# An attention kernel: VectorE's share of the exponentials regrouped from three blocks in every second job to four in every fourth, and Q transposed one job ahead instead of two

## The chip, the cores and the metric

One core of a Trainium2 chip runs the whole program. The metric is device time in microseconds (us) of one launch. The engines named below are TensorE (PE, its weight loads PEld), VectorE (DVE), ScalarE (ACT), GpSimd (POOL) and SyncE (SP). Each works through its own instructions in the order in which the program issues them, and waits on semaphores for the others.

## The reference

Grouped-query attention, batch 8, sequence 512, 32 query heads, 8 key/value heads, head size 64, all float32:

```python
K_expanded = np.repeat(K, heads_per_group, axis=2)     # 4 query heads share one key head
scores = np.einsum('bhqd,bhkd->bhqk', Q, K_expanded) * scale
weights = np.exp(scores - np.max(scores, axis=-1, keepdims=True))
weights = weights / (np.sum(weights, axis=-1, keepdims=True) + 1e-10)
output = np.einsum('bhqk,bhkd->bhqd', weights, V_expanded)
```

## The kernel before

**Jobs and blocks.** The work is 64 jobs, j = 0 to 63. A job is one key head of one batch with its four query heads, taken as two pairs of heads (i = 0, 1; `DPAIR` is pair 1). The scores of a pair are made transposed, keys on the partitions: for each of four chunks of 128 keys (kc) and each head of the pair (m) a block of 128 keys x 512 queries. A job has 16 blocks. The exponential is taken without subtracting the maximum. Checks on the sums and on V set a flag, and a general path stands behind it for inputs that need it.

**Two engines take exponentials.** ACT takes most blocks in tiles of two (`act_tile`, ACTIVATE on L217, 128 x 1024), out of a pool of two PSUM buffers (`s_ps`): PE can write tile n's scores (L199) only when ACT has finished tile n-2. DVE takes the first `taken(j)` blocks of pair 1 (kc 0 first, then kc 1) by integer arithmetic on the bits of a float16 number:

- `exp_d` (scores into `d_ps` on L199, then u, L228),
- `exp_d2` (f, L249, the low bits of u),
- g (L241) and w (L245), the correction; for jobs 3 to 62 both run on POOL,
- `exp_d4` (L262), u + w, written to the tile `pt` beside ACT's results. It is issued one job later.

`taken(j)` is 2, and 3 where `WIDE(j)` holds: the even jobs from 10 on, 27 of them. A narrow job leaves ACT seven tiles of two blocks, a wide job six and a half (its tile 4 has one block).

**Order within job j**, written out by hand in the last loop of `fast_path`; `last` is job j-1, and pv(last, i, lo, hi) are products lo to hi of the 32 that multiply pair i's weights with V (L293), in the chunk order kc 2, 3, 1, 0, so that products 0 to 15 of pair 1 need ACT's blocks alone and products 16 to 31 the chunks in which DVE has a part. PE's queue is:

1. tile 0's scores, DVE's first two blocks, tile 1's scores,
2. pv(last, 0, 0, 16), tile 2, pv(last, 0, 16, 32), tile 3,
3. eight transposes of Q (L164, `trans_q`), tile 4,
4. pv(last, 1, ...) in three pieces, with tile 5 and tile 6 between them, and DVE's third block of job j+1 after tile 5 where j+1 is wide.

DVE's queue in the same job is: u(j); a check of V in some jobs (`check_v`, L173); the normalisation of (last, 0) (reciprocal L336, multiply L340); the copy of the transposed Q out of PSUM (L167); `exp_d4(last)`; f(j); u of the third block of j+1 where j+1 is wide; the normalisation of (last, 1). POOL's queue is g(j), w(j), then the DMA issues that the program writes at the head of job j+1 (loads of Q, K and V).

**PSUM.** The eight banks are two buffers of two banks for ACT's tiles, one buffer of two banks for `d_ps` (DVE's blocks and the transposes share it, one tile after the other), and one of two banks for `pv`. As there is one `pv` buffer, pv(last, 1) starts only after the normalisation of (last, 0), and pv(j, 0) in the next job only after that of (last, 1).

**Q ahead.** Up to job 6 the Q of job j+1 is transposed in job j. Job 7 transposes Q of jobs 8 and 9, and from job 8 on it is Q of j+2, into half of a `d_ps` tile. The other half takes the third block of a wide job j+1.

Of the kernel before, what the change touches and what calls it, by code (L numbers as in the profile page):

```python
# [13 lines left out]
FP16 = mybir.dt.float16  # L14
# [3 lines left out]
ALU = mybir.AluOpType  # L18
# [6 lines left out]
EXP_K = 3.28614867e-04  # L25
EXP_F1 = 1045.05112
# [7 lines left out]
V_HI = 1.0e15  # L34


WIDE = lambda j: j >= 10 and j % 2 == 0


@with_exitstack  # L40
# [18 lines left out]
def fast_path(ctx, tc, Q, K, V, out, flag):  # L59
    nc = tc.nc  # L60
    B, S, H, D = Q.shape
# [3 lines left out]
    GP = KV // 2  # L65
# [13 lines left out]
    dve_pool = ctx.enter_context(tc.tile_pool(name="dve", bufs=2))  # L79
# [78 lines left out]
    def trans_q(j, bank, lo=0, hi=NPAIR):  # L158
        u, g = divmod(j, 2)
        ps = bank.bitcast(BF16).rearrange("p (i sc c) -> p i sc c", i=NPAIR, sc=SC)  # L160
        for i in range(lo, hi):
            for sc in range(SC):
                h = g * HPG + 2 * i
                nc.tensor.transpose(ps[:, i, sc, :], qn[u][:, sc, h:h + 2, :], ident)  # L164
        if u not in qt:
            qt[u] = qt_pool.tile([128, 2, NPAIR, S], BF16, name="qt")
        return lambda: nc.vector.tensor_copy(  # L167
            out=qt[u][:, g, lo:hi, :], in_=ps[:, lo:hi, :, :].rearrange("p i sc c -> p i (sc c)")
        )

    def check_v(b, sc):
        n = b * SC + sc
        nc.vector.tensor_reduce(  # L173
            out=okv[:, n:n + 1], in_=vt[b % 2][:, sc, :, 0:D], op=ALU.max, axis=AX.XY,
            apply_absolute_value=True,
        )
# [3 lines left out]
    NJOB = NU * 2  # L180
    DPAIR = NPAIR - 1

    def taken(j):
        return 3 if WIDE(j) else 2

    def act_tiles(j):
        every = [(i, kc, m) for i in range(NPAIR) for kc in range(SC) for m in range(2)]
        first = DPAIR * SC * 2
        mine = [n for n in range(len(every)) if not first <= n < first + taken(j)]
        groups = [[n for n in mine if n // 2 == h] for h in range(len(every) // 2)]  # L190
        return [[every[n] for n in group] for group in groups if group]

    jobs, osb, invs, ends = {}, {}, {}, []

    def scores(j, ps, i, kc, m):
        u, g = divmod(j, 2)
        b, gp = divmod(u, GP)
        keys = kt_first[:, gp, :, :] if b == 0 else kt[b][:, :, gp, :]
        nc.tensor.matmul(  # L199
            ps,  # L200
            keys[64 * m:64 * m + 64, g ^ m, kc * 128:(kc + 1) * 128],
            qt[u][64 * m:64 * m + 64, g, i, :],
            start=True,
            stop=True,
        )
# [5 lines left out]
    def act_tile(j, n):  # L211
        group = act_tiles(j)[n]
        i, kc, lo = group[0]
        ps = s_pool.tile([128, 2, S], FP32, name="s_ps")
        for _, _, m in group:
            scores(j, ps[:, m, :], i, kc, m)
        nc.scalar.activation(  # L217
            out=jobs[j]["pt"][:, i, kc, lo:, :], in_=ps[:, lo:, :], func=EXP, scale=scale
        )

    def exp_d(j, lo, hi, ps):
        st = jobs.setdefault(j, {})
        if "u" not in st:
            for name, dtype in (("u", I16), ("f", I16), ("g", BF16), ("w", BF16)):
                st[name] = dve_pool.tile([128, 3, S], dtype, name=name + "16")[:, 0:taken(j), :]
        for n in range(lo, hi):
            scores(j, ps[:, n - lo, :], DPAIR, n // 2, n % 2)
        return lambda: nc.vector.tensor_scalar(  # L228
            out=st["u"][:, lo:hi, :], in0=ps[:, 0:hi - lo, :], scalar1=A_U, scalar2=B_U,
            op0=ALU.mult, op1=ALU.add,  # L230
        )


    def by_pool(j):
        return 3 <= j < NJOB - 1

    def correction(engine, f, g, w):
        as_bits = engine is nc.gpsimd  # L240
        engine.tensor_scalar(  # L241
            out=g, in0=f, scalar1=-EXP_F1, scalar2=EXP_K * 2.0 ** (24 * as_bits),
            op0=ALU.add, op1=ALU.mult,
        )
        engine.tensor_tensor(out=w, in0=g, in1=f.bitcast(FP16) if as_bits else f, op=ALU.mult)  # L245

    def exp_d2(j):
        st = jobs[j]
        nc.vector.tensor_single_scalar(  # L249
            out=st["f"], in_=st["u"], scalar=1023, op=ALU.bitwise_and  # L250
        )
        if by_pool(j):
            exp_d3(j, nc.gpsimd)

    def exp_d3(j, engine):
        st = jobs[j]
        correction(engine, st["f"], st["g"], st["w"])

    def exp_d4(j):
        st = jobs[j]  # L260
# [17 lines left out]
    def pv(j, i, lo, hi):  # L278
        st = jobs[j]
        u, g = divmod(j, 2)  # L280
        b, gp = divmod(u, GP)
        if lo == 0:

            if j < NJOB - 1:
                t = pv_pool.tile([128, 2, S], FP32, name="pv")
            else:
                t = d_tile() if i == 0 else s_pool.tile([128, 2, S], FP32, name="s_ps")
            t = t.rearrange("p m (qc c) -> p m qc c", qc=SC)
            st["pv"][i] = t[:, :, :, 0:D + 1]
        order = blocks(j, i)  # L290
        for n in range(lo, hi):
            kc, m, qc = order[n]
            nc.tensor.matmul(  # L293
                st["pv"][i][:, m, qc, :],
                st["pt"][:, i, kc, m, qc * 128:(qc + 1) * 128],
                vt[b % 2][:, kc, 2 * gp + g, :],
                start=(n < 2 * SC and qc == 0),
                stop=(n >= len(order) - 2 * SC and qc == SC - 1),
            )
# [102 lines left out]
    bank = d_tile()  # L402
# [4 lines left out]
    bank = d_tile()  # L407
    trans_q(0, bank[:, 0, :], 0, 1)()


    for j in range(NJOB):
        end = j == NJOB - 1
        last = j - 1
        late = last >= 0
        u, g = divmod(j, 2)
        b, gp = divmod(u, GP)
        open_job(j)
        if j == 1:

            nc.gpsimd.tensor_copy(out=gate, in_=jobs[0]["pt"][0:1, 0, SC - 1, 0, 0:1])  # L420
            load_q(2)
            load_q(3)
        if g == 0 and u >= 1 and u + 3 < NU:
            load_q(u + 3)
        if (gp, g) == (1, 0) and b + 1 < B:
            load_k(b + 1)
        if 3 <= 2 * gp + g < 3 + SC and b + 1 < B:
            load_v(b + 1, chunks=(2 * gp + g - 3,))
        if gp == 2 and g == 0 and b + 1 < B:
            dma_k(b + 1)  # L430

        cut = (4, 18) if taken(j) > 2 else (11, 19)
        act_tile(j, 0)
        if j == 0:
            trans_q(0, bank[:, 1, :], 1, NPAIR)()
            act_tile(j, 1)
            exp_d(j, 0, 2, d_tile())()
        else:
            exp_d(j, 0, 2, d_tile())()
            act_tile(j, 1)  # L440

        if j == 8:
            check_v(0, 0)
        if g == (b < B - 1) and j > 1:
            check_v(b, gp)
        if late:
            pv(last, 0, 0, 16)
        act_tile(j, 2)
        if late:
            pv(last, 0, 16, 32)  # L450
            norm(last, 0)
        act_tile(j, 3)

        reads = []
        if not end:
            bank = d_tile()

            ahead = (j + 1,) if j < 7 else (8, 9) if j == 7 else (j + 2,)
            for n, to in enumerate(ahead):
                if to < NJOB:  # L460
                    reads.append(trans_q(to, bank[:, n, :]))
            if j == 1:
                for swap in range(2):
                    reads.append(first_k(1, swap, bank[:, 1, swap * S // 2:]))
            elif j > 1 and b == 0 and gp + 1 < GP:
                reads.append(first_k(gp + 1, g, bank[:, 1, :]))
        else:
            pv(j, 0, 0, 16)
        for read in reads:
            read()  # L470

        if late and by_pool(last):
            exp_d4(last)
        check_sums()
        exp_d2(j)
        if not by_pool(j):
            exp_d3(j, nc.vector)
            exp_d4(j)
        act_tile(j, 4)
        if late:  # L480
            pv(last, 1, 0, cut[0])
        act_tile(j, 5)
        if not end and taken(j + 1) > 2:
            exp_d(j + 1, 2, taken(j + 1), bank[:, 1:2, :])()
        if late:
            pv(last, 1, *cut)
        act_tile(j, 6)
        if late:
            pv(last, 1, cut[1], 32)
            norm(last, 1)  # L490
            del jobs[last]
        if end:
            pv(j, 0, 16, 32)
            norm(j, 0)
            pv(j, 1, 0, 32)
            norm(j, 1)
# [118 lines left out]
```

## Time and profile before

| | |
|---|---|
| median of 3 runs | 423.37 us (422.98 to 424.95) |
| the profiled execution, its own time | 423.68 us |
| its span, first to last instruction | 422.0 us |
| ACT busy | 404.2 us, 96% of the span |
| PE busy | 385.7 us, 91% |
| DVE busy | 344.9 us, 82% |
| POOL busy | 291.8 us, 69% |
| mean granted TensorE clock | 0.984 |

The page of the profile gives each engine's busy time, the chain of work that ended last, and groups of like instructions with the mean duration of one and the idle time ahead of them with its releaser. Matmuls and activations are pipelined, so that their records overlap, and a mean duration of ACT (1086 ns for a tile of two blocks) is longer than the distance from one to the next. The timeline lists the instructions in order of time: start in us, duration in us, engine, line, operation, tiles, count, and in brackets the idle time before it with its releaser.

### The profile page before, as it was taken

Reading aid. Unit: us, or ns where it says so; the run is one execution under the profiler, and the core shown is the slowest. Engines: PE = TensorE matmul, PEld = TensorE weight load, DVE = VectorE, ACT = ScalarE, POOL = GpSimd, SP = SyncE. Lnnn points to the kernel's source line nnn. Section 1 sums busy time; section 2 is a strip of 40 time slices with the busy share of each in tenths; the row PEclk is TensorE's granted clock in tenths of the full one; section 3 lists DMA queues with packets and bytes.
Section 4 is the critical chain, followed back from the end, with each engine's and each line's share of the span. In section 5 each row is a group of like instructions: output and inputs, shape, how many; then the busy total and the mean of one; then the engine's idle time right before and its main releaser. Section 6 shows DMA issues by size and latency. Waiting matters only on the chain.

```text
span 422.0 us, 13063 instructions
## 1 busy us (share of the span) xinstructions
PE 385.7 (91%) x5689; PEld 233.6 (55%) x5689; DVE 344.9 (82%) x611; ACT 404.2 (96%) x449; POOL 291.8 (69%) x209
## 2 busy tenths in 40 slices
PE   6889999999999999999999999999999999999983
PEld 2446565555555555555555555555555555555552
DVE  2697788889888888888888888888989888898875
ACT  3899999999999999999999999999999999999992
POOL 8504656778758876787866887677885887666560
PEclk9599999999999999999999999999999999999998
DMA  9996986599967998499964999649996799642223
GB/s 97 177 139 159 217 165 151 70 207 187 191 151 99 216 198 160 133 198 133 229 150 116 206 163 255 157 69 200 157 225 155 122 206 207 148 123 101 102 91 115
DMA packets 91438, 66.95 MB, mean 159 GB/s; under 512 B 52080, under 2 KB 74608, under 8 KB 91376
## 3 DMA queue, kind: packets, MB, share of 16 engines
q0 software_dynamic: 56544, 25.17, 51.1%
q1 hardware_dynamic: 34832, 40.90, 34.5%
q8 instruction: 45, 0.74, 0.7%
q14 instruction: 17, 0.14, 0.1%
HBM read 50.33 MB, written 33.55 MB: 199 GB/s over the span
## 4 chain that ended last, share of the span: by engine, by line
ACT 54%; PE 36%; DVE 6%; issue 1%; POOL 1%; ACTq 0%; DVEq 0%; POOLq 0%
ACT pt L217 54%; PE s_ps L199 17%; PE pv L293 16%; PE d_ps L199 1%; DVE o_sb L340 1%; PE d_ps L164 1%; DVE pt L262 1%; DVE u L228 1%; DVE qt L167 1%; DVE w L245 0%; POOL q_nat L126 0%; DVE kt_first L146 0%; ACTq L217 0%; PE d_ps L143 0%; DVE f L249 0%
## 5 line engine op out<-in xcount | busy, mean ns | idle before, releaser
L217 ACT ACTIVATE pt<-s_ps 128x1024 f16<-128x1024 f32 (+1 forms) x448 | 402.9, 1066 | 9.1 <-PE s_ps L199 9.0
L293 PEld LDWEIGHTS <-pt 128*128 128x128 f16 x4096 | 144.2, 98 | 86.8 <-issue 50.4
L293 PE MATMUL pv<-v,pt 128*128 128x65 bf16 x4032 | 183.2, 195 | 2.6 <-DVE o_sb L340 1.6
L199 PE MATMUL s_ps<-qt,kt 64*128 64x512 bf16 x757 | 152.7, 384 | 19.9 <-ACT pt L217 15.4
L245 POOL TENSOR_TENSOR w<-g,f 128x1024 bf16<-128x1024 bf16 (+1 forms) x60 | 153.7, 2562 | 5.0
L241 POOL TENSOR_SCALAR g<-f 128x1024 bf16<-128x1024 int16 (+1 forms) x60 | 73.9, 1231 | 110.1 <-DVE f L249 110.1
L228 DVE TENSOR_SCALAR u<-d_ps 128x1024 int16<-128x1024 f32 (+1 forms) x91 | 96.2, 1058 | 1.1 <-PE d_ps L199 1.1
L340 DVE TENSOR_TENSOR o_sb<-pv,inv 128x512 f32<-128x512 f32 x125 | 86.5, 692 | 4.5 <-DVE inv L336 0.2
L199 PEld LDWEIGHTS <-kt 64*128 64x128 bf16 x896 | 49.0, 93 | 62.6 <-issue 35.0
L336 DVE RECIPROCAL inv<-pv 128x8 f32<-128x8 f32 x125 | 25.9, 207 | 55.8 <-PE pv L293 55.4
L262 DVE TENSOR_TENSOR pt<-u,w 128x1536 uint16<-128x1536 int16 (+1 forms) x64 | 50.9, 795 | 0.2
L167 DVE COPY qt<-d_ps 128x1024 bf16<-128x1024 bf16 (+1 forms) x65 | 44.3, 683 | 4.5 <-PE d_ps L164 2.9
L164 PE MATMUL d_ps<-ident,q_nat 128*128 128x128 bf16 x512 | 40.1, 222 | 1.1 <-DVE kt_first L146 0.9
L164 PEld LDWEIGHTS <-q_nat 128*128 128x128 bf16 x512 | 29.2, 98 | 15.8 <-issue 15.7
L199 PE MATMUL d_ps<-qt,kt 64*128 64x512 bf16 x139 | 31.4, 376 | 0.3
L249 DVE TENSOR_SCALAR f<-u 128x1536 int16<-128x1536 int16 (+1 forms) x64 | 30.8, 481 | 0.0
L111 POOL DMA_DIRECT2D v<-in_V_dram x32 | 29.0, 910 | 0.4 <-issue 0.4
L126 POOL DMA_DIRECT2D q_nat<-in_Q_dram x34 | 27.4, 806 | 1.5 <-DMA q_nat<-in_Q_dram 1.3
L199 PE MATMUL s_ps<-qt,kt_first 64*128 64x512 bf16 x112 | 23.7, 419 | 4.1 <-ACT pt L217 3.0
L173 DVE TENSOR_REDUCE okv<-v 128x1 f32<-128x512 bf16 x32 | 21.6, 675 | 0.0
L199 PEld LDWEIGHTS <-kt_first 64*128 64x128 bf16 x128 | 8.0, 95 | 12.2 <-issue 8.4
L103 POOL DMA_DIRECT2D k_nat<-in_K_dram x10 | 7.7, 770 | 1.0 <-POOLq L599 0.8
(40 smaller groups left out, 37.6 us busy)
## 6 DMA issues: line engine op xcount, KB each, us to landing
out_dram<-o_sb SPq DMA_DIRECT2D x31, 1024.0 KB, 6.9
q_nat<-in_Q_dram POOLq DMA_DIRECT2D x31, 512.0 KB, 6.3
k_nat<-in_K_dram POOLq DMA_DIRECT2D x7, 512.0 KB, 8.6
v<-in_V_dram POOLq DMA_DIRECT2D x28, 128.0 KB, 7.6
kt<-kt SPq DMA_DIRECT2D x14, 256.0 KB, 4.6
out_dram<-o_sb SPq DMA_DIRECT2D x4, 256.0 KB, 2.4
kt<-k_nat SPq DMA_TRANSPOSE x28, 5.6
v<-in_V_dram POOLq DMA_DIRECT2D x4, 96.0 KB, 7.8
```

What stands on the lines that cost most here:

```text
L111: nc.gpsimd.dma_start(out=vt[b % 2][:, sc, lo:hi, 0:D], in_=V[b, sc * 128:(sc + 1) * 128, lo:hi, :],)
L164: nc.tensor.transpose(ps[:, i, sc, :], qn[u][:, sc, h:h + 2, :], ident)
L167: return lambda: nc.vector.tensor_copy(out=qt[u][:, g, lo:hi, :], in_=ps[:, lo:hi, :, :].rearrange("p i sc c -> p i (sc c)"))
L199: nc.tensor.matmul(ps, keys[64 * m:64 * m + 64, g ^ m, kc * 128:(kc + 1) * 128], qt[u][64 * m:64 * m + 64, g, i, :], start=True, stop=True,)
L217: nc.scalar.activation(out=jobs[j]["pt"][:, i, kc, lo:, :], in_=ps[:, lo:, :], func=EXP, scale=scale)
L228: return lambda: nc.vector.tensor_scalar(out=st["u"][:, lo:hi, :], in0=ps[:, 0:hi - lo, :], scalar1=A_U, scalar2=B_U, op0=ALU.mult, op1=AL ...
L241: engine.tensor_scalar(out=g, in0=f, scalar1=-EXP_F1, scalar2=EXP_K * 2.0 ** (24 * as_bits), op0=ALU.add, op1=ALU.mult,)
L245: engine.tensor_tensor(out=w, in0=g, in1=f.bitcast(FP16) if as_bits else f, op=ALU.mult)
L249: nc.vector.tensor_single_scalar(out=st["f"], in_=st["u"], scalar=1023, op=ALU.bitwise_and)
L262: nc.vector.tensor_tensor(out=st["pt"][:, DPAIR, :, :, :].rearrange("p kc m q -> p (kc m) q")[:, 0:n, :].bitcast(U16), in0=st["u"], in1=st ...
L293: nc.tensor.matmul(st["pv"][i][:, m, qc, :], st["pt"][:, i, kc, m, qc * 128:(qc + 1) * 128], vt[b % 2][:, kc, 2 * gp + g, :], start=(n < 2 ...
L340: nc.vector.tensor_tensor(out=osb[u][:, :, h:h + 2, :].rearrange("p qc m d -> p m qc d"), in0=sums[:, :, :, 0:D], in1=inv[:, :, :, None].t ...
```

## The change

Where DVE takes more than two blocks, it takes four, so two whole key chunks of pair 1; and it does so in jobs 6, 10, 14, ..., 62, which are 15 jobs. A wide job leaves ACT six whole tiles, and there is no half tile any more. In a wide job g runs on DVE instead of POOL (w stays on POOL). Its blocks 3 and 4 are made one job earlier, as the third was, in the whole `d_ps` tile that held the transposes. Q of job j+1 is transposed in job j throughout. The checks of V stand in jobs 0, 3, 4, 7 of the eight jobs of a batch (3, 4, 7, 7 in the first batch, 0, 3, 4, 4 in the last). The pieces of pv(last, 1) are cut anew: two of 16 in a wide job, 11 + 8 + 13 ahead of a wide job, 11 + 11 + 10 otherwise.

```diff
-WIDE = lambda j: j >= 10 and j % 2 == 0
+WIDE = lambda j: j >= 6 and j % 4 == 2
...
     def taken(j):
-        return 3 if WIDE(j) else 2
+        return 4 if WIDE(j) else 2
...
-                st[name] = dve_pool.tile([128, 3, S], dtype, name=name + "16")[:, 0:taken(j), :]
+                st[name] = dve_pool.tile([128, 4, S], dtype, name=name + "16")[:, 0:taken(j), :]
...
     def exp_d2(j):
         st = jobs[j]
         nc.vector.tensor_single_scalar(
             out=st["f"], in_=st["u"], scalar=1023, op=ALU.bitwise_and
         )
+        scales = nc.gpsimd if by_pool(j) and taken(j) == 2 else nc.vector
+        scales.tensor_scalar(
+            out=st["g"], in0=st["f"], scalar1=-EXP_F1, scalar2=EXP_K * 2.0 ** (24 * by_pool(j)),
+            op0=ALU.add, op1=ALU.mult,
+        )
         if by_pool(j):
-            exp_d3(j, nc.gpsimd)
+            nc.gpsimd.tensor_tensor(
+                out=st["w"], in0=st["g"], in1=st["f"].bitcast(FP16), op=ALU.mult
+            )
+        else:
+            nc.vector.tensor_tensor(out=st["w"], in0=st["g"], in1=st["f"], op=ALU.mult)
...
+    v_checks = {}
+    for b in range(B):
+        places = (3, 4, 7, 7) if b == 0 else (0, 3, 4, 4) if b == B - 1 else (0, 3, 4, 7)
+        for sc, place in enumerate(places):
+            v_checks.setdefault(2 * GP * b + place, []).append((b, sc))
...
-        cut = (4, 18) if taken(j) > 2 else (11, 19)
         act_tile(j, 0)
...
-        if j == 8:
-            check_v(0, 0)
-        if g == (b < B - 1) and j > 1:
-            check_v(b, gp)
+        for b_, sc in v_checks.get(j, ()):
+            check_v(b_, sc)
...
             bank = d_tile()
-
-            ahead = (j + 1,) if j < 7 else (8, 9) if j == 7 else (j + 2,)
-            for n, to in enumerate(ahead):
-                if to < NJOB:
-                    reads.append(trans_q(to, bank[:, n, :]))
+            reads.append(trans_q(j + 1, bank[:, 0, :]))
...
-        act_tile(j, 4)
+
+        more = not end and taken(j + 1) > 2
+        cuts = (0, 16, 32) if taken(j) > 2 else (0, 11, 19, 32) if more else (0, 11, 22, 32)
+        for n, (lo, hi) in enumerate(zip(cuts[:-1], cuts[1:])):
+            act_tile(j, 4 + n)
+            if more and n == 1:
+                exp_d(j + 1, 2, taken(j + 1), bank)()
+            if late:
+                pv(last, 1, lo, hi)
         if late:
-            pv(last, 1, 0, cut[0])
-        act_tile(j, 5)
-        if not end and taken(j + 1) > 2:
-            exp_d(j + 1, 2, taken(j + 1), bank[:, 1:2, :])()
-        if late:
-            pv(last, 1, *cut)
-        act_tile(j, 6)
-        if late:
-            pv(last, 1, cut[1], 32)
             norm(last, 1)
```

## The prediction

> **What bounds the kernel now.** First the page's engine lines and groups, with forms kept apart, then the waits.
>
> ```profile
> PE 385.7 (91%) x5689; PEld 233.6 (55%) x5689; DVE 344.9 (82%) x611; ACT 404.2 (96%) x449; POOL 291.8 (69%) x209
> ```
>
> ```profile
> L217 ACT ACTIVATE pt<-s_ps 128x1024 f16<-128x1024 f32 x421 | 390.0, 1086 | 9.1 <-PE s_ps L199 9.0
> L245 POOL TENSOR_TENSOR w<-g,f 128x1536 bf16<-128x1536 bf16 x27 | 83.6, 3095 | 2.2
> L228 DVE TENSOR_SCALAR u<-d_ps 128x1024 int16<-128x1024 f32 x64 | 77.7, 1215 | 1.1 <-PE d_ps L199 1.1
> L245 POOL TENSOR_TENSOR w<-g,f 128x1024 bf16<-128x1024 bf16 x33 | 70.1, 2125 | 2.8
> L217 ACT ACTIVATE pt<-s_ps 128x512 f16<-128x512 f32 x27 | 20.3, 753 | 0.0
> L249 DVE TENSOR_SCALAR f<-u 128x1024 int16<-128x1024 int16 x37 | 15.9, 429 | 0.0
> L249 DVE TENSOR_SCALAR f<-u 128x1536 int16<-128x1536 int16 x27 | 15.0, 554 | 0.0
> ```
>
> ```profile
> PE s_ps L199 <- ACT pt L217: 18.4, 60, 0.7
> ACT pt L217 <- PE s_ps L199: 9.0, 8, 6.2
> ```
>
> ACT sat idle only 9.0 us, 6.2 of them at the start: it is the bound, and PE waits for its buffers. The single records of L217 give the pace. In steady state one full tile ends 0.917 us after the other, a narrow job takes 6.417, a wide one 6.085. The half tile itself adds 0.490, but the tile behind it 1.013: its scores can start only once ACT has finished the tile ahead of the half one, and 0.39 of matmul plus semaphores is as long as the half tile. So a half tile costs 0.585, not 0.458.
>
> PE keeps little in hand. From the timeline's steps: two score blocks 0.32 (0.22 if more scores follow), 16 products 0.59, that is 0.030 each and 0.12 for the last one to drain, eight transposes 0.55. A tile with its work is 0.91 of PE against 0.917 of ACT. Scores must start 0.54 before ACT ends the tile ahead (0.44 until they are readable, 0.10 for a tile that starts unpipelined), or ACT stalls. Job 63, the last one, shows the price:
>
> ```profile
> 407.15 3.10 POOL L245 TENSOR_TENSOR w<-g,f 128x1536 bf16<-128x1536 bf16 x1
> 411.49 0.96 DVE L262 TENSOR_TENSOR pt<-u,w 128x1536 uint16<-128x1536 int16 x1
> 411.63 0.33 PE L293 MATMUL pv<-v,pt 128*128 128x65 bf16 x5
> 412.51 0.27 PE L293 MATMUL pv<-v,pt 128*128 128x65 bf16 x3 [0.55 <-DVE pt L262]
> 412.70 0.39 PE L199 MATMUL s_ps<-qt,kt 64*128 64x512 bf16 x2
> ```
>
> `exp_d4` of wide job 62 ends at 412.45. PE's product 16, the first that needs it, stands ahead of tile 6's scores and waits 0.55. ACT ends tile 5 at 413.09, so the limit is 413.09 - 0.54 = 412.55; the scores start at 412.70; the record of tile 6 ends 0.154 late. One late sum of DVE passes through PE to ACT.
>
> **The change, part by part.**
>
> ACT: jobs 6 to 62 before took 356.88 us (end of job 5's last tile, 50.71, to job 62's, 407.59). After, undisturbed: 15 wide jobs x 6 x 0.917 = 82.5 and 42 narrow x 6.417 = 269.5, together 352.0. The gain to be had is 4.9.
>
> DVE, new sizes: f of 128x2048 by the step from 429 to 554 is 0.68; g on DVE has only 128x1024 (428 ns, four times), so by f's step 0.69; u of two blocks 1.22 in place of 0.69; `exp_d4` by 682 and 949 is 1.22. Bounds: f 0.55 to 0.86, g 0.43 to 0.86 (two blocks; twice that), `exp_d4` 0.95 to 1.36. POOL: w by 2125 and 3095 is 4.06, at least 3.10 and at most two of 128x1024, 4.25. I take the straight lines, since two rows of each kind fix f, `exp_d4` and w.
>
> The job ahead of a wide one: u grows by 0.53, but the `exp_d4` in front is of a narrow job (0.68 for 0.95), so u ends about 0.25 later, as PE reaches the next job's DVE blocks. Nothing waits yet.
>
> Now the wide job and the one behind it, with 0 at the wide job's first scores. ACT ends the job before at 0.86 and the wide job at 6.36. PE runs at ACT's pace (transposes 3.07, tile 5 at 4.58), and the next job's scores start at 5.50. DVE: copy 3.73, `exp_d4` of the job before 4.34, f 4.93 to 5.62, g 5.54 to 6.22 (records overlap by 0.08). Two things hang on g:
>
> - The normalisation of (last, 1) stands behind it. Its products are done at 5.57, its reciprocal starts at 6.13, and it ends at 7.07. PE's first product of the next job needs that `pv` buffer and waits until 7.13 in place of 6.74.
> - w starts on POOL at 6.31 and ends at 10.37. Before, f to w's end took 5.3; now 5.44, but the job in between is 0.59 shorter.
>
> The job behind: PE's delay shifts its tile 2 to 7.70 (ACT stalls 0.05), and DVE's chain with it: u 6.98 to 8.20, the V check to 8.8, normalisation to 9.64, copy 9.58 to 10.27. `exp_d4` of the wide job could start at 10.18, waits for w until 10.46, and ends at 11.68. PE reached product 16 at 10.68. The new cut is 11 to 22, so products 16 to 21 stand ahead of tile 6: they run from 11.73, and tile 6's scores start at 12.01. ACT ended tile 5 at 11.91, 0.05 late. The limit was 11.91 - 0.54 = 11.37. Stall 0.64, with the 0.05 0.69 a cycle of four jobs. ACT has nothing in reserve, so it counts in full.
>
> Sum: wide jobs 6 to 58 have their followers in 7 to 59, 14 stalls. Job 7 has two V checks: the second (0.59) puts back the normalisation, so tile 5 (stall 0.26), and `exp_d4`, which ends at 12.0 (stall 0.67); with the 0.05 that is 0.98. 13 x 0.69 + 0.98 = 9.95. 352.0 + 9.95 - 356.88 = **+5.1**. The end: `exp_d4(62)` ended 4.86 after ACT's job 62 before and would end 5.36 after it now; the rest of the tail hangs on it, so +0.5. With the profiled execution's 423.68 (span 422.0 and 1.7 around it) that is 429.3. This execution lies 0.3 above the median of 423.37, so I say **429.0**.
>
> At nothing: Q one job ahead. The copy ends at -1.99, and the first reader (DVE's blocks 3 and 4) is reached at -1.62; jobs 4 to 6, which work one ahead already, take 6.417 each without a stall. That cover is 0.37; gone, PE and then ACT wait 15 times for what exceeds it. The moved checks of V (0.68 each) lie in jobs where DVE has some slack, but those in jobs 3 and 7 of a batch stand behind a wide job and are in the layout above. POOL loses 15 g and 27 half-sizes, and its DMA issues stand behind w: w(wide) ends at 10.37, two issues of 0.9 end at 12.2, and the next g is called for at 12.1, so it may start 0.1 late against some 3 us of slack.
>
> On w the Trainium skill speaks against the change more than the rows do. "GPSIMD Engine Reference", section 3.1, gives 2.6 cycles an element for two-input operations and 4497 ns at 2048 elements; by that, an estimate, w would end 0.43 later than I have it, and the total would be 435. The rows here (2125 and 3095) lie below that line, so they decide.
>
> **The rivals.**
>
> - *The whole gain* (faster). Price and point: everything as above, but `exp_d4` of the wide job ends by 11.0 in place of 11.68, so that product 16 is no brake; then 423.4 - 4.9 = 418.5. With w at 3.1, g at 0.43 and `exp_d4` at 0.95 together this is what comes out; gain and loss are even at a stall of 0.3 a cycle. For it: POOL is 69% busy, DVE 82%. Against it: means; the rows scale by elements and three low ends at once are unlikely.
> - *Half of it*. One low end alone (w under 3.8, g at 0.43, or `exp_d4` at 0.95) takes 0.25 off each stall: 3.6 less, 425.4. A little more and nothing is seen.
> - *Heavier*. w at 4.25 or g at 0.86 adds 0.18 to each stall: 431.5; all three high, 0.5: 436. The skill's rule on w falls in here.
> - *Q one ahead is late*: copy delayed over 0.37 by DVE's load in the job ahead; 0.2 more, 15 times, is 432. Against it: that job's DVE rows (two u, two normalisations at 0.9, copy, `exp_d4`, f) add up to 6.0 of 6.417.
>
> **How the numbers follow.** Forecast 0.66, half of it 0.13, the whole gain 0.07, heavier 0.10, Q late 0.04. A measurement of this kernel tells about 0.5% (2.1 us) from no change. Faster takes the whole gain and a tail of the second, 0.08; same, the rest of the second, 0.12; slower 0.80. The range goes from 423.5 (inside the second case) to 434.0 (between the single high ends and all of them) and leaves out the whole gain and the far end, under 2 in 10.
>
> **What would show it.** Wide jobs take 5.50 on ACT and those behind them about 7.1, the others 6.42; PE waits about 1 us for L262 once in four jobs, between tile 5 and tile 6; PE's waits for L340 grow by 0.4 in the same job; w 4.06 on POOL, g on DVE 0.69. I am wrong if `exp_d4` of 128x2048 starts before POOL is done with other work in hand (w much shorter than 4 us), or if jobs other than those behind a wide one exceed 6.42.

## The result and the profile after

The changed kernel takes 434.31 us (median of 4 runs, 433.74 to 434.97), the one before 423.18 beside it: ratio 1.0257, 95% interval 1.0222 to 1.0293. It is slower by 11 us. The forecast was slower, at 429.0, with a range of 423.5 to 434.0; the time lies 0.3 above the range. The profiled execution took 434.47 with a span of 432.7.

The engine lines of the page:

```profile
PE 376.1 (87%) x5689; PEld 233.5 (54%) x5689; DVE 356.8 (82%) x614; ACT 402.7 (93%) x434; POOL 268.0 (62%) x194
```

ACT issues 15 instructions less and is busy 1.5 us less, in a span that is 10.7 longer. Only DVE got more work, 11.9 us of it (344.9 before); ACT and PE have less to do, and wait. The view of the waits says where (us in all, times, longest):

```profile
ACT pt L217 <- PE s_ps L199: 20.6, 31, 6.5
...
PE pv L290 <- DVE o_sb L337: 12.8, 27, 0.9
PE pv L290 <- DVE pt L259: 12.4, 15, 1.6
```

The last two read like this in the kernel before:

```profile
PE pv L293 <- DVE o_sb L340: 1.6, 3, 0.9
...
PE pv L293 <- DVE pt L262: 0.7, 2, 0.6
```

Before, ACT waited 9.0 us in 8 places, 6.2 of it at the start. Now it is 31 places, and PE, which stands ahead of ACT, waits 15 times for `exp_d4` (now L259; one wait for each wide job) and 27 times for a normalisation (L337). The groups of the new sizes:

```profile
L250 POOL TENSOR_TENSOR w<-g,f 128x2048 bf16<-128x2048 bf16 x15 | 60.9, 4061 | 39.7 <-DVE g L245 39.7
L259 DVE TENSOR_TENSOR pt<-u,w 128x2048 uint16<-128x2048 int16 x15 | 18.4, 1225 | 1.4
L245 DVE TENSOR_SCALAR g<-f 128x2048 bf16<-128x2048 int16 x15 | 10.4, 694 | 0.5
L241 DVE TENSOR_SCALAR f<-u 128x2048 int16<-128x2048 int16 x15 | 10.3, 686 | 0.0
```

w was put at 4.06, `exp_d4` at 1.22, g at 0.69 and f at 0.68: the straight lines held. Now the timeline of wide job 30, which starts at 205.21, and of job 31 behind it, which starts at 211.63. First the wide job:

```profile
210.16 0.69 DVE L241 TENSOR_SCALAR f<-u 128x2048 int16<-128x2048 int16 x1
210.88 0.69 DVE L245 TENSOR_SCALAR g<-f 128x2048 bf16<-128x2048 int16 x1
211.49 0.20 DVE L333 RECIPROCAL inv<-pv 128x8 f32<-128x8 f32 x1
211.63 0.39 PE L199 MATMUL s_ps<-qt,kt 64*128 64x512 bf16 x2 [0.30 <-ACT pt L217]
211.66 4.06 POOL L250 TENSOR_TENSOR w<-g,f 128x2048 bf16<-128x2048 bf16 x1 [2.51 <-DVE g L245]
211.73 0.69 DVE L337 TENSOR_TENSOR o_sb<-pv,inv 128x512 f32<-128x512 f32 x1
...
212.48 0.66 PE L290 MATMUL pv<-v,pt 128*128 128x65 bf16 x16 [0.45 <-DVE o_sb L337]
```

f, g and the normalisation stand in one queue; PE gets its `pv` buffer at 212.48. Then the job behind, up to tile 6:

```profile
215.61 0.39 PE L199 MATMUL s_ps<-qt,kt 64*128 64x512 bf16 x2
215.76 1.23 DVE L259 TENSOR_TENSOR pt<-u,w 128x2048 uint16<-128x2048 int16 x1
215.93 0.33 PE L290 MATMUL pv<-v,pt 128*128 128x65 bf16 x5
216.90 0.42 DVE L241 TENSOR_SCALAR f<-u 128x1024 int16<-128x1024 int16 x1
217.04 0.35 PE L290 MATMUL pv<-v,pt 128*128 128x65 bf16 x6 [0.78 <-DVE pt L259]
217.33 0.39 PE L199 MATMUL s_ps<-qt,kt 64*128 64x512 bf16 x2
...
217.76 12.94 ACT L217 ACTIVATE pt<-s_ps 128x1024 f16<-128x1024 f32 x14 [0.49 <-PE s_ps L199]
```

POOL's w ends at 215.72, `exp_d4` starts at 215.76, products 16 to 21 wait for it, tile 6's scores come at 217.33, and ACT stands idle 0.49 and pays another 0.1 for an unpipelined start. From the single ACT records, a wide job takes 5.50 us, jobs two and three behind it 6.41 to 6.42, as forecast; the job directly behind takes about 7.20 and 7.47 by turns, where 7.1 was forecast (job 7, which was laid out by itself, takes 7.84). Its tile 2 ends 0.19 or 0.46 late, its tile 6 0.60.

The 10.7 us of span go like this: jobs 6 to 62 +8.89 (365.77 for 356.88); job 63 and what follows it +1.35; jobs 0 to 5 +0.45. The last is not the change: in the profiles of all these kernels job 5 ends anywhere from 50.0 to 51.7, and in this one the granted clock rose at 20.1 in place of 19.3.

### The profile page after: what moved, and what is told of

The parts are those of the page before. It is cut to its first block, busy times and chain, and to the rows that moved or that the text cites. A ratio compares the mean times of both kernels' runs of the same rounds, so it can differ in the third digit from the quotient of the medians.

```text
span 432.7 us, 13038 instructions
## 1 busy us (share of the span) xinstructions
PE 376.1 (87%) x5689; PEld 233.5 (54%) x5689; DVE 356.8 (82%) x614; ACT 402.7 (93%) x434; POOL 268.0 (62%) x194
## 4 chain that ended last, share of the span: by engine, by line
ACT 28%; PE 23%; DVE 21%; POOL 18%; issue 9%; ACTq 0%; POOLq 0%; DVEq 0%
ACT pt L217 28%; POOL w L250 13%; PE pv L290 10%; PE s_ps L199 10%; DVE pt L259 7%; DVE o_sb L337 4%; DVE f L241 2%; DVE g L245 2%; POOL q_nat L126 2%; POOL g L245 1%; POOL k_nat L103 1%; PE d_ps L199 1%; DVE inv L333 1%; DVE ok L301 1%; PE d_ps L164 1%
## 5 line engine op out<-in xcount | busy, mean ns | idle before, releaser
L217 ACT ACTIVATE pt<-s_ps 128x1024 f16<-128x1024 f32 x433 | 401.4, 1097 | 21.4 <-PE s_ps L199 20.6
L290 PE MATMUL pv<-v,pt 128*128 128x65 bf16 x4032 | 178.8, 195 | 25.2 <-DVE o_sb L337 12.8
L250 POOL TENSOR_TENSOR w<-g,f 128x1024 bf16<-128x1024 bf16 (+1 forms) x60 | 156.7, 2611 | 43.4 <-DVE g L245 39.7
L199 PE MATMUL s_ps<-qt,kt 64*128 64x512 bf16 x756 | 147.9, 383 | 16.2 <-ACT pt L217 10.9
L245 POOL TENSOR_SCALAR g<-f 128x1024 bf16<-128x1024 int16 x45 | 46.8, 1041 | 105.6 <-DVE f L241 105.6
L228 DVE TENSOR_SCALAR u<-d_ps 128x1024 int16<-128x1024 f32 x79 | 95.9, 1214 | 1.1 <-PE d_ps L199 1.1
L337 DVE TENSOR_TENSOR o_sb<-pv,inv 128x512 f32<-128x512 f32 x125 | 86.4, 691 | 4.5 <-DVE inv L333 0.2
L259 DVE TENSOR_TENSOR pt<-u,w 128x1024 uint16<-128x1024 int16 (+1 forms) x64 | 51.8, 809 | 1.7
L241 DVE TENSOR_SCALAR f<-u 128x1024 int16<-128x1024 int16 (+1 forms) x64 | 30.8, 482 | 0.0
L199 PE MATMUL d_ps<-qt,kt 64*128 64x512 bf16 x140 | 27.1, 376 | 2.0 <-DVE u L228 2.0
L245 DVE TENSOR_SCALAR g<-f 128x2048 bf16<-128x2048 int16 (+1 forms) x19 | 12.2, 641 | 0.7
```

Source lines behind the costliest of these rows:

```text
L199: nc.tensor.matmul(ps, keys[64 * m:64 * m + 64, g ^ m, kc * 128:(kc + 1) * 128], qt[u][64 * m:64 * m + 64, g, i, :], start=True, stop=True,)
L217: nc.scalar.activation(out=jobs[j]["pt"][:, i, kc, lo:, :], in_=ps[:, lo:, :], func=EXP, scale=scale)
L228: return lambda: nc.vector.tensor_scalar(out=st["u"][:, lo:hi, :], in0=ps[:, 0:hi - lo, :], scalar1=A_U, scalar2=B_U, op0=ALU.mult, op1=AL ...
L241: nc.vector.tensor_single_scalar(out=st["f"], in_=st["u"], scalar=1023, op=ALU.bitwise_and)
L245: scales.tensor_scalar(out=st["g"], in0=st["f"], scalar1=-EXP_F1, scalar2=EXP_K * 2.0 ** (24 * by_pool(j)), op0=ALU.add, op1=ALU.mult,)
L250: nc.gpsimd.tensor_tensor(out=st["w"], in0=st["g"], in1=st["f"].bitcast(FP16), op=ALU.mult)
```

## The experiments

The theory after the result: two waits through PE to ACT. One goes through w and `exp_d4` to tile 6. The other goes through f and g, the normalisation and the `pv` buffer to tile 2. Rival A: DVE simply has too much to do, and its lateness would turn up wherever it is let. Rival B: Q transposed one ahead is late. Ratios are to the kernel before, measured beside each.

**Late products behind tile 6.**

```diff
+        if late and taken(last) > 2:
+            cuts = (0, 11, 16, 32)
```

> The changed kernel with one edit: in the job behind a wide one the pieces of pv(last, 1) are cut at 11 and 16 in place of 11 and 22, so that the products which need the late sum of DVE stand behind tile 6's scores. Theory (the late sum holds up tile 6 by 0.60 us in each of 14 jobs): that stall goes, the next job's tile 0 can just be reached in time, 14 x 0.60 = 8.4 us less, about 426. Rival A (DVE is simply overloaded, and the lateness turns up at the next tile instead): 432 to 434. Rival B (Q transposed one ahead is the cost): no change, 434.

426.01 us, ratio 1.006 (1.0043 to 1.0077). Its timeline in the job behind a wide one:

```profile
212.84 1.23 DVE L259 TENSOR_TENSOR pt<-u,w 128x2048 uint16<-128x2048 int16 x1
213.02 0.33 PE L290 MATMUL pv<-v,pt 128*128 128x65 bf16 x5
213.49 0.39 PE L199 MATMUL s_ps<-qt,kt 64*128 64x512 bf16 x2
213.99 0.42 DVE L241 TENSOR_SCALAR f<-u 128x1024 int16<-128x1024 int16 x1
214.12 0.66 PE L290 MATMUL pv<-v,pt 128*128 128x65 bf16 x16 [0.24 <-DVE pt L259]
```

The sum is as late as it was, but tile 6's scores (213.49) no longer stand behind it. Added over jobs 6 to 62, the stall at tile 6 falls from 8.47 us to nothing, 0.51 comes back at the next job's tile 0, and the 4.9 at tile 2 stay. So PE's order turned DVE's lateness into ACT's, and A and B fall for this part.

**Q one ahead, alone, in the kernel before.**

```diff
-            ahead = (j + 1,) if j < 7 else (8, 9) if j == 7 else (j + 2,)
-            for n, to in enumerate(ahead):
-                if to < NJOB:
-                    reads.append(trans_q(to, bank[:, n, :]))
+            reads.append(trans_q(j + 1, bank[:, 0, :]))
```

> The kernel before with one part of the change alone: Q of job j+1 is transposed in job j throughout, three blocks in every second job as before. Theory (four blocks in one job make the late sum, Q has no part in it): no change, 422.5 to 424. Rival B (the copy of Q is late where the wide job's third block is waiting for it): 0.2 us or more in each of 27 jobs, 428 or more.

423.97 us, ratio 1.0013 (1.0001 to 1.0024). Jobs 6 to 62 take 356.79 in its profile, 356.88 before. Rival B falls; what is left of the ratio is under what can be told. This kernel has three blocks in a wide job; with four, the kernel without stalls further down works one ahead too.

**g of the wide jobs back on POOL.**

```diff
-        scales = nc.gpsimd if by_pool(j) and taken(j) == 2 else nc.vector
+        scales = nc.gpsimd if by_pool(j) else nc.vector
```

> The changed kernel with g of the wide jobs back on POOL. Theory (two waits, one through g in front of the normalisation on DVE, one through w on POOL): the stall at tile 2 behind a wide job (0.19 and 0.46 by turns) goes, and w ends 1.25 us later because g takes about 1.9 on POOL, which goes into tile 6 in full: 1.25 more in each of 14 jobs and at the end, about 452. Rival A (DVE's load is the cause): DVE is relieved by 0.7 in each wide job, so about 430.

466.14 us, ratio 1.1008 (1.099 to 1.1027). Relieving DVE made it much slower, so A falls; the stall at tile 2 went, as expected, which says that it came from g on DVE. But the expectation was short by 14 us. Timeline of the job behind a wide one:

```profile
227.75 0.33 PE L290 MATMUL pv<-v,pt 128*128 128x65 bf16 x5
229.14 1.23 DVE L259 TENSOR_TENSOR pt<-u,w 128x2048 uint16<-128x2048 int16 x1 [1.88 <-POOL w L250]
230.28 0.42 DVE L241 TENSOR_SCALAR f<-u 128x1024 int16<-128x1024 int16 x1
230.43 0.46 PE L290 MATMUL pv<-v,pt 128*128 128x65 bf16 x6 [2.35 <-DVE pt L259]
```

PE now idles 2.35 us, and the view of the windows shows what follows. Its columns are the window, its length, busy time of PE, PEld, DVE, ACT and POOL (with the number of instructions), the mean granted clock, and two of the DMA:

```profile
226.00:229.40 3.40, 1.99 (x28) 1.28 (x28) 1.52 (x3) 3.21 (x4) 3.11 (x1) 1.00 0.63 240
229.40:232.50 3.10, 2.07 (x22) 1.18 (x23) 1.64 (x4) 1.02 (x1) 1.62 (x2) 0.68 0.00 0
232.50:239.40 6.90, 6.49 (x92) 3.84 (x89) 5.79 (x11) 6.68 (x8) 3.76 (x4) 0.90 0.53 76
```

The 0.68 and 0.90 are means over stretches of full and of half clock: by the trace's clock records the clock is halved for 3.4 or 6.8 us from about the end of each of these gaps (2.3 to 2.6 us long, 14 of them), here from 230.52 to 233.94. The next job stalls too: jobs 6 to 62 take 45 us more than ACT's own 352.0, and 10.9 of them lie there, which the expectation did not have. The other 3 or so beyond it lie at tile 6, whose scores come at half clock (0.61 for two in place of 0.39). In the changed kernel PE's longest wait for `exp_d4`, 1.6 us in job 63, leaves the clock at 1.00. The Trainium skill, "TensorE: Matmul & The Clock Gate", Part 1, says that half clock follows an idle window of about 3.4 us; here gaps well below that were enough each time, and the measurement decides.

**The last sum in halves, key chunk 1 first.**

```diff
-        nc.vector.tensor_tensor(
+        for lo, hi in ((2, 4), (0, 2)) if n > 2 else ((0, 2),):
+            nc.vector.tensor_tensor(
...
-            in0=st["u"],
-            in1=st["w"],
+                in0=st["u"][:, lo:hi, :],
+                in1=st["w"][:, lo:hi, :],
```

> The changed kernel with the last sum of a wide job (u + w) made in two halves, key chunk 1 first, which PE needs first. Theory: products 16 to 21 can go 0.54 us earlier, the stall at tile 6 falls from 0.60 to about 0.06, DVE has 0.14 more to do: 14 x 0.54 = 7.6 us less, about 427. Rival A (DVE's load): 434 to 436, since DVE gets more to do. Rival B (Q one ahead): 434.

426.2 us, ratio 1.0075 (1.0054 to 1.0095). DVE does more and the kernel is 8 us faster than the changed one. The stall at tile 6 fell from 8.47 us to 0.96 over jobs 6 to 62.

**The check of the sums moved.**

```diff
-        check_sums()
+        if j % 4 == 0:
+            check_sums()
```

> The changed kernel with the check of the sums (two operations on L301 every eighth job, which fall into the job ahead of every second wide one) moved three jobs on. Theory: that pair of 0.29 us is why the stall at tile 2 behind a wide job is 0.46 in every second cycle and 0.19 in the others; moved, all show 0.19, 7 x 0.27 = 1.9 us less, about 432.4. If the two values have another reason (the batch, the loads): no change, 434.

433.06 us, ratio 1.0227 (1.021 to 1.0244). In the records 13 of the 14 wide jobs now have 0.19 to 0.20 at tile 2 behind them; over jobs 6 to 62 the tile 2 stall falls from 4.87 to 3.05. That settles where the 0.46 came from: two operations of 0.29 us in every eighth job push u of blocks 3 and 4, and all of DVE's queue in the wide job, back. The exception is wide job 6: tile 2 of job 7 keeps its 0.49. No check of the sums stands ahead of it, but a copy of K out of PSUM does (L146, 0.41 us in job 5), as ahead of no other wide job; that this is the reason was not tested.

**f early.**

```diff
-    def exp_d2(j):
+    def exp_f(j):
...
+    def exp_d2(j):
+        st = jobs[j]
+        if taken(j) == 2:
+            exp_f(j)
...
             check_v(b_, sc)
+        if taken(j) > 2:
+            exp_f(j)
```

> The changed kernel with one instruction moved: in a wide job f stands on DVE right behind the first u (and the V checks), where DVE waits 0.8 us for PE, in place of standing behind the copy and the sum of the job before. DVE does the same work. Theory (f and g hold up the normalisation by 0.7, and w on POOL by as much): the stall at tile 2 goes, the sum of the wide job starts about 0.45 to 0.6 earlier, so the stall at tile 6 falls to about 0.1, the end gains 0.6: 434.3 - 14 x 0.8 - 0.6 = about 422.5 (421.5 to 424). Rival A (DVE overloaded by the amount of work): 432 or more. Should f be held up by POOL, which runs w at that time, it shows as a longer f in the record.

424.87 us, ratio 1.0023 (1.0011 to 1.0035), 9.4 us faster than the changed kernel with the same instructions. Tile 2 has no stall left (4.87 to none that counts). Tile 6 kept 3.9 of 8.47 us: 0.07 behind one half of the wide jobs, 0.4 behind those with the check of the sums in front, and 0.66 in job 7, where I had expected 0.1. So 2.4 us of my expectation were missing.

**f early, late products behind tile 6, check of the sums moved.**

> The changed kernel with f early in the wide jobs, the pieces of pv(last, 1) cut at 11 and 16 behind a wide job, and the check of the sums moved to jobs with slack. Theory: no stall is left between jobs 6 and 62, so ACT's own time counts, 4.9 us under the kernel before there; the end keeps up to 1.5 us of loss: 419 to 421. Rival A: 425 or more.

419.89 us, ratio 0.9916 (0.9893 to 0.9938): faster than both kernels. Jobs 6 to 62 take 352.34, where ACT's own time is 352.0. Its page and its waits:

```profile
PE 374.0 (89%) x5689; PEld 236.6 (57%) x5689; DVE 358.6 (86%) x614; ACT 399.5 (95%) x434; POOL 268.7 (64%) x194
```

```profile
ACT pt L217 <- PE s_ps L199: 9.0, 7, 6.4
...
PEld L295 <- DVE pt L264: 5.4, 16, 1.0
```

PE's weight loads still wait for the sum 16 times, but behind tile 6, where it costs ACT nothing. DVE is busier than in the changed kernel by 1.8 us.

**w and the last sum in halves.**

```diff
-            nc.gpsimd.tensor_tensor(
-                out=st["w"], in0=st["g"], in1=st["f"].bitcast(FP16), op=ALU.mult
-            )
+            for lo, hi in ((2, 4), (0, 2)) if taken(j) > 2 else ((0, 2),):
+                nc.gpsimd.tensor_tensor(
+                    out=st["w"][:, lo:hi, :],
...
```

The last sum is cut in halves as above.

> The changed kernel with w on POOL and the last sum on DVE of a wide job both made in halves, key chunk 1 first. Two readings differ. If DVE's sum (two inputs from SBUF) can run beside POOL's second half of w: the first half sum starts at about 10.2 after the wide job's first scores in place of 10.55 and lasts 0.68; stall at tile 6 nil, 425 to 425.5. If such an operation of DVE is held up while POOL works (as the one on L301 in job 63 seems to be, 0.91 us in place of 0.26): the record of the first half sum is longer than 0.68 and ends only some 0.4 to 0.6 after POOL's w, and the time is that of the kernel with the sum alone split, 426 to 427.

426.49 us, ratio 1.0066 (1.0049 to 1.0083), the time of the kernel with the sum alone split. The first half's record lasts 0.85 in 13 wide jobs where 0.68 is its length, and it ends 0.55 after POOL's w (in the other two, 6 and 62, it starts after w's end). So having half of w early buys nothing, as DVE's sum is held up until POOL is through. It started too close to w's end to show a longer hold; the last section has one of 2.4 us.

## Why the prediction was wrong

The direction and the mechanism were right; the size was half. The profiled execution took 434.47 where the sum gave 429.3. Of the 5.2 between them, tile 2 is 4.2, the end 0.85, jobs 0 to 5 0.45 and jobs 6 and 18 0.2, while tile 6 came out 0.5 under its term. By its own steps:

- *ACT undisturbed, 352.0 in jobs 6 to 62; a half tile costs 0.585.* Right: 352.34 in the kernel that has no stalls left.
- *The new durations.* Right within 0.01 us: 4.061, 1.225, 0.694, 0.686.
- *w and `exp_d4` hold up tile 6 by 0.64.* Right: 0.60 (8.47 us in all), and the cut and the split of the sum take it away.
- *The `pv` buffer holds up tile 2 by 0.05.* This is the step that failed, by its size: 0.19 and 0.46, 4.87 us in all where 0.7 was in the sum. Two things were left out. I let g start 0.08 before f ends, as instructions of DVE that do not depend on each other do; but g reads f, and starts 0.03 after f ends (210.16 + 0.69, then 210.88), as the multiply does behind its reciprocal. The kernel before showed it too: in its job 63 f ends at 412.79 and g on DVE starts at 412.82. That is 0.11 of the 0.14 by which PE got its buffer later than laid out (7.27 after the wide job's start for 7.13), on a chain with no slack. And I did not count the check of the sums, two operations of 0.29 us in the job ahead of every second wide one: 0.27 more in the job behind, seven times. The run with the check moved shows this second part; the first is read from the records, and f early takes both away.
- *Job 7: 0.98.* Measured 1.42: tile 2 has 0.49 where 0.05 was put, and tiles 5 and 6 have 0.25 and 0.66, as laid out. Job 6 and job 18, not in the sum, stall 0.1 each.
- *The end: +0.5.* Measured +1.35. In job 63 the check of the sums runs before the last sum, and now at the same time as POOL's w, which ends 0.8 later in the job than before (4.1 after its first scores, 3.3 before). Its first operation took 0.91 us where 0.26 is its length before:

```profile
420.28 1.21 DVE L301 SCALAR_TENSOR_TENSOR ok<-inv,ok 128x104 f32<-128x104 f32 x2
```

  It ended 0.12 after w (417.01 + 4.06 = 421.07), and `exp_d4(62)` and all of the tail came 0.65 later for that. This is read from the records; no run moved that check. The other 0.2 of the difference is not traced.
- *Q one ahead at nothing.* Right: alone it leaves jobs 6 to 62 as they were, and the kernel without stalls has it too.
- *The range.* Its heavy end was worked out from durations, which held; the order of events on DVE, where a wide job has no slack left, had no term in it.

What stays open is small: the 0.1 at tile 2 of jobs 6 and 18, what lies behind job 7's 0.49, and 0.2 at the end. The rest of the difference is told by records and by the kernels above.

## What to carry to other kernels

Where the bound engine has no reserve, write out the queue of each helper engine for one period and count every instruction in it, those of every eighth job too, and take a dependent instruction as starting after the one it reads, not beside its end. When several blocks are gathered into one bigger step, their result comes later as a whole, and what counts is what stands behind the waiting instruction in the next engine's queue: here moving six products behind the next scores, or one instruction into a gap, was worth 8 to 9 us, while relieving the engine that looked overloaded cost 32.

## What the runs showed of the hardware that was not expected

VectorE was held by GpSimd until GpSimd's instruction was through. Three kinds of VectorE instruction started while POOL ran w and ended a fixed time after it: `scalar_tensor_tensor` on 104 columns 0.12 after (0.91 in place of 0.26), the sum u + w on 1024 columns 0.55 after (0.85 in place of 0.68), and f on 2048 columns, in the kernel with f early, 0.55 after (0.72 to 0.76 in place of 0.69). In each case that is the instruction's own length less 0.13 to 0.14, so nearly all of it ran after w. The longest hold stands in job 63 of the kernel with g back on POOL:

```profile
448.86 4.06 POOL L250 TENSOR_TENSOR w<-g,f 128x2048 bf16<-128x2048 bf16 x1
450.36 2.99 DVE L301 SCALAR_TENSOR_TENSOR ok<-inv,ok 128x104 f32<-128x104 f32 x2
```

The first of the two operations starts 2.56 us before w ends at 452.92, and its single record lasts 2.69, to 0.13 after w. Not every instruction is held: the multiply of the normalisation, with one input in PSUM, took its usual 0.69 inside w, 45 times in the changed kernel. The Trainium skill, "SBUF — State Buffer", section "SBUF: two separate sides", says that VectorE with two SBUF inputs or in a two-port mode and GpSimd share a port pair that one of them holds for the whole instruction. The records of the two kinds with two inputs agree; f has one input, and no run here shows in which mode it ran. This belonged into the prediction, since the change makes w longer and moves it towards VectorE's sums.

TensorE's clock was halved after idle gaps of 2.3 to 2.6 us, as told above, and not after one of 1.6: a wait of the longer kind costs more than itself.
